# Weight sums and splits of the output products on pairs of tiles, temporaries in pools of each phase

## The chip, the cores and the metric

One core of one Trainium2 chip. The program is launched once; the metric is the device time of the launch in microseconds (us), median of three runs. TensorE (PE) multiplies, VectorE (DVE), ScalarE (ACT) and GpSimd (POOL) do the work on elements, and SyncE's queue (SP) issues most transfers. Each engine runs its instructions in the order in which the program lists them.

## The reference

Two residual layers on x[512 tokens, 2048]: a gated linear recurrence (mixer A, 16 heads of 128), then attention with forget gates (mixer B, 16 heads of 128). The change touches the last line of each layer, the output product:

```python
# layer A
h = rmsnorm(x, norm_w);  proj = h @ w_in            # queries, forget gates, values, gate
o = hgrn2_chunkwise(q, k, i, log_f)
o = head_rmsnorm(o, out_norm_w) * silu(gate)
x = x + o @ w_out                                    # [512, 2048] @ [2048, 2048]
# layer B
k, v, F = shared_kv(x, ...)
o = forgetting_attention(q, k, v, F)
o = head_rmsnorm(o, out_norm_w) * silu(gate)
x = x + o @ w_out
```

All is float32. The kernel splits each operand of a product in two float32r parts, a high and a low one (x = xh + xl, w = wh + wl), and adds three products: wh xh, wh xl, wl xh.

## The kernel before

**Tiling.** Everything is kept feature-major: a tile has 128 features as partitions and the 512 tokens as columns. A contraction over 2048 features has 16 tiles (kt = 0 to 15). A plain group (`group`) makes four output tiles at once, in four PSUM banks gm0 to gm3: for each kt one weight tile 128x512 is loaded (`Chunks.load`, SP queue, 256 KB, three buffers wr), split by a cast on ScalarE (wh) and a subtraction on VectorE (wl; both in `split`, L420 and L421), and used by twelve matmuls of 512 columns (L217 to L219 where the weights are stationary). Between the steps of a group the program interleaves the mixers of the heads (`pump`).

**Phases.** Phase "a" runs mixer A and its projections. The output product of A follows: its tiles 0 to 3 as one plain group, while the last heads finish (`out_product`), and its tiles 4 to 15 in "quick" form, phase "oa". Then phase "b" for mixer B, a plain group, and phase "ob" for the quick part of B's output product, which ends the program.

**The quick form.** Six groups u = 0 to 5 make two output tiles each, by Winograd's form of Strassen's product: seven products of half-size blocks in place of eight. Weight and operand are cut into four blocks (A11 to A22; B11 to B22). For each p = 0 to 7, a pair of contraction tiles p and p + 8, there is one weight tile 128x512 that holds the four blocks, and 21 matmuls of 256 columns (L268 to L270: seven products of three parts), so 168 a group. A group accumulates in four banks, gm and mx in turn. Around it stand:
- `w_sums` (L134 to L137) makes the four sums wm of the weight blocks: three additions on POOL and one on VectorE, 128x128 each, for each weight tile. `w_split_quick` then casts and subtracts the blocks (128x384) and the sums (128x512) into w7h and w7l.
- `quick_prep` (L234 to L237) makes, once for each p, the four sums tm of the operand's blocks: three on VectorE, one on POOL (L235), 128x256 each; then it splits the first into the place of half an operand tile (xh, xl) and the other three into th and tl (128x768). These serve all six groups. tm has one buffer. Preparations 0 to 3 are traced ahead of the plain group's last contraction tile, 4 to 7 in the first quick group.
- `quick_sum` (L278 to L289) puts the seven products of a group together and adds the residual: a copy on ScalarE, eleven operations of 256 columns on VectorE.
- The plain group's four banks are emptied by L806 (in A, result y) and L988 (in B, result z).

**What sets the order.** The program is traced in the order of the Python code, and the tile framework then schedules it: a simulated timeline decides, for each engine, in which order its instructions are listed. What it may move depends on the buffers: a tile that takes the space of another has to wait for it. Tiles of a mixer or of a quick product live in a pool of the phase (`mt`), opened by `phase`; those that live through all phases (t, wh, wl, wr, sl, vh, vl, the operands xh and xl, the y) in one pool of the program (`nt`). The space of a phase's pool is used again by the next phase's.

Of the kernel before, what the change touches and what calls it, by code (L numbers as in the profile page):

```python
# [15 lines left out]
P = 128  # L16
T = 512
# [14 lines left out]
def hgrn2_fox(ctx, tc, io):  # L32
# [24 lines left out]
    def tmp():  # L57
        return nt("t", (P, T), 4)
# [4 lines left out]
    def mt(tag, shape, bufs=1, dt=F32):  # L63
        """A tile of the phase's mixer."""
        return nt(tag, shape, bufs, dt, cur["sb"])

# [5 lines left out]
    def pump(n):  # L72
        """Trace n steps of the first two tasks in turn; the second starts when the first is halfway."""
# [56 lines left out]
    def w_sums(r):  # L130
        """Of the blocks A21, A11, A12, A22 the four sums of Winograd's form."""
        a21, a11, a12, a22 = (r[:, i * P : (i + 1) * P] for i in range(4))
        m = mt("wm", (P, 4, P), 2)
        G.tensor_add(m[:, 0, :], a21, a22)  # L134
        G.tensor_sub(m[:, 2, :], a11, a21)  # L135
        G.tensor_sub(m[:, 1, :], m[:, 0, :], a11)  # L136
        V.tensor_sub(m[:, 3, :], a12, m[:, 1, :])  # L137
        return m

    def w_split_quick(r, m):  # L140
        """A11, A12, A22 and the sums."""
        h = mt("w7h", (P, 7, P), 2, F32R)
        l = mt("w7l", (P, 7, P), 2, F32R)
        split(r[:, P:T].rearrange("p (a c) -> p a c", c=P), h[:, 0:3, :], l[:, 0:3, :])
        split(m, h[:, 3:7, :], l[:, 3:7, :])
        return h, l

    class Chunks:
        """The weight tiles of all groups in the order of their use."""
# [6 lines left out]
        def add(self, ap, scales):  # L156
            for kt in range(KT):
                self.todo.append((ap[kt], None, lambda r, m, kt=kt: w_split(r, kt, scales)))

        def add_quick(self, ap):  # L160
            for kt in range(KT // 2):
                self.todo.append((ap[kt], w_sums, w_split_quick))

        def load(self):
            if not self.todo:
                return
            ap, sums, fn = self.todo.pop(0)
            r = nt("wr", (P, T), 3)
            nc.sync.dma_start(r, ap)
            self.raw.append([r, sums, fn, None])  # L170

        def sums(self, n):
            for c in self.raw[:n]:
                if c[1] and cur["quick"]:
                    c[3] = c[1](c[0])
                    c[1] = None

        def split(self):
            if not self.raw:
                return  # L180
            self.sums(1)
            r, _, fn, m = self.raw.pop(0)
            self.parts.append(fn(r, m))
            self.sums(1)

        def take(self):
            while len(self.parts) < 2 and self.raw:
# [11 lines left out]
    def group(evac, token_major=False, rate=3, before=None):  # L199
        """Four accumulations over the contraction, one per bank."""  # L200
        banks = [nt(f"gm{j}", (P, T), 1, pool=ps) for j in range(4)]
        for kt in range(KT):
            wts.load()
            if before:
                before(kt)
            wts.split()
            h, l = wts.take()
            for j in range(4):
# [866 lines left out]
```

## Time and profile before

| | us |
|---|---|
| median of three runs | 2034.12 (2033.39 to 2034.17) |
| the profiled execution, first to last instruction | 2033.7 |
| A: first quick matmul, last matmul of group u = 4 | 911.75, 1023.1 |
| B: first quick matmul, last matmul | 1899.18, 2026.6 |

The times of the stretches come from one profiled execution. In the rows of the profile, `out<-in` names a tile that is written and those that are read (`w7l<-wr,w7h` is the low part of a quick weight), a bracket gives the idle time ahead of an instruction and what ended it, and L is the line in the kernel.

The six quick groups of A's product take 22.1, 22.0, 22.8, 22.6 and 22.2 us for u = 0 to 4, counted from the start of one to the start of the next; those of B's 22.9, 20.8, 21.3, 21.4, 20.4 and 20.8 us.

### The profile page before, as it was taken

Reading aid. Unit: us, or ns where it says so; the run is one execution under the profiler, and the core shown is the slowest. Engines: PE = TensorE matmul, PEld = TensorE weight load, DVE = VectorE, ACT = ScalarE, POOL = GpSimd, SP = SyncE. Lnnn points to the kernel's source line nnn. Section 1 sums busy time; section 2 is a strip of 40 time slices with the busy share of each in tenths; the row PEclk is TensorE's granted clock in tenths of the full one; section 3 lists DMA queues with packets and bytes.
Section 4 is the critical chain, followed back from the end, with each engine's and each line's share of the span. In section 5 each row is a group of like instructions: output and inputs, shape, how many; then the busy total and the mean of one; then the engine's idle time right before and its main releaser. Section 6 shows DMA issues by size and latency. Waiting matters only on the chain. (4 is left out here: it accounts for less than half of the span.)

```text
span 2033.7 us, 30490 instructions
## 1 busy us (share of the span) xinstructions
PE 1986.5 (98%) x10202; PEld 1693.6 (83%) x10202; DVE 1587.4 (78%) x3346; ACT 1142.1 (56%) x2408; POOL 481.1 (24%) x692
## 2 busy tenths in 40 slices
PE   7999999999999999989989999999999999999898
PEld 6888888888888888879987888888888888888898
DVE  8878987989799889798985667666766676687877
ACT  5656665667567465654453655554555456566443
POOL 8303210314033031147740000010001000011565
PEclk9999999999999999999999999999999999999999
DMA  5322222222222222244443333323323322323453
GB/s 174 84 82 83 68 84 78 79 78 78 78 80 71 82 80 78 89 118 137 147 125 89 94 94 88 91 87 99 92 85 94 94 89 88 92 80 107 132 157 114
DMA packets 107501, 195.14 MB, mean 96 GB/s; under 512 B 12992, under 2 KB 13120, under 8 KB 107344
## 3 DMA queue, kind: packets, MB, share of 16 engines
q1 hardware_dynamic: 107200, 193.19, 31.9%
q8 instruction: 80, 1.31, 0.3%
q14 instruction: 77, 0.63, 0.1%
q10 hardware_dynamic: 144, 0.01, 0.0%
HBM read 184.73 MB, written 8.42 MB: 95 GB/s over the span
## 5 line engine op out<-in xcount | busy, mean ns | idle before, releaser
L217 PE MATMUL gm<-xh,wh 128*128 128x512 f32 x1664 | 652.0, 392 | 6.8 <-ACT wh L420 6.6
L218 PE MATMUL gm<-xl,wh 128*128 128x512 f32 x1664 | 651.6, 392 | 0.0
L219 PE MATMUL gm<-xh,wl 128*128 128x512 f32 x1664 | 614.9, 392 | 6.3 <-DVE wl L421 5.8
L217 PEld LDWEIGHTS gm<-xh,wh 128*128 128x128 f32 x1664 | 313.6, 189 | 70.9 <-ACT wh L420 7.0
L219 PEld LDWEIGHTS gm<-xh,wl 128*128 128x128 f32 x1664 | 311.9, 188 | 70.9 <-DVE wl L421 7.2
L218 PEld LDWEIGHTS gm<-xl,wh 128*128 128x128 f32 x1664 | 313.6, 188 | 63.2
L421 DVE TENSOR_TENSOR wl<-wr,wh 128x512 fp32r<-128x512 f32 x288 | 216.6, 756 | 68.1 <-ACT wh L420 59.3
L420 ACT CAST wh<-wr 128x512 fp32r<-128x512 f32 x288 | 177.4, 620 | 150.5 <-PE gm L218 108.6
L125 DVE SCALAR_TENSOR_TENSOR wl<-wr,v_b_norm_w,wh 128x256 fp32r<-128x256 f32 (+1 forms) x192 | 113.1, 590 | 134.3 <-ACT wh L124 123.1
L124 ACT ACTIVATE wh<-wr,v_b_norm_w 128x256 fp32r<-128x256 f32 (+1 forms) x192 | 111.9, 585 | 181.7 <-PE gm L218 133.9
L214 PE MATMUL gm<-wl,xh 128*128 128x512 f32 x512 | 201.5, 394 | 0.0
L215 PE MATMUL gm<-wh,xl 128*128 128x512 f32 x512 | 200.0, 391 | 0.0
L213 PE MATMUL gm<-wh,xh 128*128 128x512 f32 x512 | 184.9, 392 | 1.1 <-DVE z L542 0.9
L919 POOL TENSOR_SCALAR_AFFINE_SELECT s<-s 128x128 f32<-128x128 f32 x64 | 27.5, 430 | 644.9 <-DVE s L918 644.2
L124 ACT ACTIVATE wh<-wr,v_kv_norm_w 128x256 fp32r<-128x256 f32 (+1 forms) x192 | 110.3, 574 | 59.0 <-PE gm L215 35.1
L125 DVE SCALAR_TENSOR_TENSOR wl<-wr,v_kv_norm_w,wh 128x256 fp32r<-128x256 f32 (+1 forms) x192 | 111.2, 581 | 35.7 <-ACT wh L124 35.1
L568 DVE COPY_PREDICATED at<-m,mx 128x128 f32<-128x128 uint8 (+3 forms) x448 | 109.6, 296 | 8.1 <-PE mx L575 7.6
L213 PEld LDWEIGHTS gm<-wh,xh 128*128 128x128 f32 x512 | 96.0, 188 | 21.1 <-DVE z L542 1.3
L214 PEld LDWEIGHTS gm<-wl,xh 128*128 128x128 f32 x512 | 96.3, 188 | 18.5 <-DVE wl L421 0.4
L215 PEld LDWEIGHTS gm<-wh,xl 128*128 128x128 f32 x512 | 96.2, 188 | 18.6
L370 POOL TENSOR_TENSOR z<-z,t 128x512 f32<-128x512 f32 x32 | 49.7, 1568 | 208.2 <-ACT t L369 208.1
L420 ACT CAST w7h<-wm 128x512 fp32r<-128x512 f32 x96 | 59.5, 620 | 66.0 <-DVE wm L137 65.3
(239 smaller groups left out, 4121.9 us busy)
## 6 DMA issues: line engine op xcount, KB each, us to landing
wr<-in_wa_qf SPq DMA_DIRECT2D x128, 256.0 KB, 2.6
wr<-in_wb_qk SPq DMA_DIRECT2D x128, 256.0 KB, 2.6
wr<-in_wa_v SPq DMA_DIRECT2D x64, 256.0 KB, 2.6
wr<-in_wa_g SPq DMA_DIRECT2D x64, 256.0 KB, 2.6
wr<-in_wb_v SPq DMA_DIRECT2D x64, 256.0 KB, 2.6
wr<-in_wb_g SPq DMA_DIRECT2D x64, 256.0 KB, 2.6
wr<-in_wa_q SPq DMA_DIRECT2D x48, 256.0 KB, 2.6
wr<-in_wb_q SPq DMA_DIRECT2D x48, 256.0 KB, 2.7
```

The lines of the kernel that those rows point to most:

```text
L124: S.activation(h[:, c], r[:, c], AF.Copy, scale=w[:, kt : kt + 1])
L125: V.scalar_tensor_tensor(l[:, c], r[:, c], w[:, kt : kt + 1], rd(h)[:, c], op0=ALU.mult, op1=ALU.subtract)
L213: PE.matmul(banks[j], xh, h, start=f, stop=False)
L214: PE.matmul(banks[j], xh, l, start=False, stop=False)
L215: PE.matmul(banks[j], xl, h, start=False, stop=e)
L217: PE.matmul(banks[j], h[:, c], Xh[kt], start=f, stop=False)
L218: PE.matmul(banks[j], h[:, c], Xl[kt], start=False, stop=False)
L219: PE.matmul(banks[j], l[:, c], Xh[kt], start=False, stop=e)
L370: G.tensor_mul(z, z, l)
L420: S.copy(h, src)
L421: return V.tensor_sub(l, src, rd(h))
L568: V.copy_predicated(out, mv, data)
```

## The change

- **Weight sums.** Two weight tiles are taken at a time. The sums are written in another, equivalent form of the seven products, so that all four come out of three VectorE additions on views of both tiles: one of 2x256 columns and two of 2x128 (L146 to L148). POOL has none of them left. The order of the blocks in the weights' memory layout changes with it.
- **Pairs of weight tiles.** All weights, those of the mixers too, come in loads of 512 KB for two tiles; wr has two buffers of that size in place of three of half. Quick weights are split in pairs (2x384 and 2x512 columns), into tiles wh and wl of two pairs. Lines: the matmuls of the plain group are L227 to L229, the quick ones L282 to L284, the split is L432 and L433, `quick_prep` L244 to L247, the evacuations L811 and L993.
- **Sums of the products.** `quick_sum` takes whole banks: a copy of 512 columns on ScalarE and seven operations on VectorE, three of 256 and four of 512 columns (L291 to L301).
- **Pools.** The temporaries t, sl, wh, wl, vh and vl are now allocated in the phase's pool, and the pools are opened with waits for single tiles. The mixers' pr has one buffer in place of two, and the norm's sum of squares takes the buffer of rstd.
- **Start.** The input tiles and the first weights are fetched in the order x0, x1, w0 and w1 together, x2, x3, instead of x0, w0, x1, w1, x2, w2, x3.

In numbers of instructions: POOL 698 before, 410 after; VectorE 3290 and 3201; ScalarE 2348 and 2251; DMAs issued by SP 749 and 429; matmuls the same.

```diff
@@ tmp, phase
     def tmp():
-        return nt("t", (P, T), 4)
+        return mt("t", (P, T), 4)
...
+        cur["sb"] = c.enter_context(tc.tile_pool(name=f"sb{name}", bufs=1, reuse_waits="tile"))
...
-        cur["sb"] = c.enter_context(tc.tile_pool(name=f"sb{name}", bufs=1))
@@ weights
+    def w_tiles(shape):
+        n = 2 if cur["quick"] else 3
+        return mt("wh", shape, n, F32R), mt("wl", shape, n, F32R)
...
     def w_sums(r):
-        a21, a11, a12, a22 = (r[:, i * P : (i + 1) * P] for i in range(4))
-        m = mt("wm", (P, 4, P), 2)
-        G.tensor_add(m[:, 0, :], a21, a22)
-        G.tensor_sub(m[:, 2, :], a11, a21)
-        G.tensor_sub(m[:, 1, :], m[:, 0, :], a11)
-        V.tensor_sub(m[:, 3, :], a12, m[:, 1, :])
+        m = mt("wm", (P, 2, 4, P), 2)
+        V.tensor_add(m[:, :, 0:2, :], r[:, :, 2:4, :], view(r, 0, [[4 * P, 2], [0, 2], [1, P]]))
+        V.tensor_add(m[:, :, 2, :], m[:, :, 0, :], r[:, :, 3, :])
+        V.tensor_add(m[:, :, 3, :], m[:, :, 2, :], r[:, :, 1, :])
         return m
...
-        split(r[:, P:T].rearrange("p (a c) -> p a c", c=P), h[:, 0:3, :], l[:, 0:3, :])
-        split(m, h[:, 3:7, :], l[:, 3:7, :])
-        return h, l
+        split(r[:, :, 1:4, :], h[:, :, 0:3, :], l[:, :, 0:3, :])
+        split(m, h[:, :, 3:7, :], l[:, :, 3:7, :])
+        return [(h[:, i, :, :], l[:, i, :, :]) for i in range(2)]
...
-            r = nt("wr", (P, T), 3)
+            r = nt("wr", (P, 2 * T), 2)
@@ quick_prep
-        G.tensor_sub(m[:, 2, :], b22, b12)
+        G.tensor_sub(m[:, 2, :], b12, b22)
         V.tensor_sub(m[:, 1, :], b22, m[:, 0, :])
-        V.tensor_sub(m[:, 3, :], m[:, 1, :], b21)
+        V.tensor_sub(m[:, 3, :], b21, m[:, 1, :])
@@ quick_sum
-        S.copy(u2, P1)
-        V.tensor_add(o1[:, lo], P1, r1[:, lo])
...
-        V.scalar_tensor_tensor(o2[:, lo], P4, -1.0, o2[:, lo], op0=ALU.mult, op1=ALU.add)
+        S.copy(e, p16)
+        V.tensor_sub(u, e[:, :TN], e[:, TN:])
+        V.tensor_sub(e[:, TN:], u, p45[:, TN:])
+        V.tensor_sub(u, p7[:, :TN], u)
+        V.tensor_add(e, p23, e)
+        d = tmp()
+        V.tensor_add(
+            d.rearrange("p (a c) -> p a c", a=2), p45.rearrange("p (a c) -> p a c", a=2), view(u, 0, [[0, 2], [1, TN]])
+        )
+        V.tensor_add(o1, e, r1)
+        V.tensor_add(o2, d, r2)
@@ Norm, mixers, start
-            self.acc = nt("vh", (P, T), 1)
+            self.acc = nt("rstd", (P, T), 1)
...
-        pr = mt("pr", (P, NW, 192), 2)
+        pr = mt("pr", (P, NW, 192), 1)
...
-    for kt in range(3):
+    for kt in range(2):
         fetch_x()
-        wts.load()
+    wts.load()
+    fetch_x()
     fetch_x()
```

How the order changes on VectorE is shown at three places. In the rows, the first number behind a name counts tiles.

The first is the end of A's plain group. Before, the evacuations L806 of its banks stand behind the preparation of p = 6 (tl6), and those of p = 0 to 5 stand further up, among the plain group's weight splits (wl):

```order
L236 TENSOR_TENSOR tm_2057_10111<-y14_1730_8512,tm_2057_10111 128x256
L421 TENSOR_TENSOR xl6_1967_9712<-tm_2057_10111,xh6_1966_9711 128x256
L237 TENSOR_TENSOR tm_2057_10111<-tm_2057_10111,y14_1730_8512 128x256
L421 TENSOR_TENSOR w7l_2047_10033<-wm_2028_9972,w7h_2046_10032 128x512
L137 TENSOR_TENSOR wm_2048_10038<-wr_2010_9907,wm_2048_10038 128x128
L421 TENSOR_TENSOR tl6_2059_10117<-tm_2057_10111,th6_2058_10116 128x768
L806 TENSOR_TENSOR y0_2029_9980<-gm0_1931_9573,z_1927_9565 128x512
L234 TENSOR_TENSOR tm_2064_10156<-y7_961_4690 128x256
L137 TENSOR_TENSOR wm_2055_10083<-wr_2042_10019,wm_2055_10083 128x128
L806 TENSOR_TENSOR y1_2030_9987<-gm1_1932_9574,z_1928_9567 128x512
```

In the changed program, the same place: the plain group's last two weight splits are wl_1867 and wl_1872, and the first row of the first preparation (tm_1875, of p = 0) comes next. L811 is the evacuation, wr_1868 and wr_1903 are the first two pairs of quick weights:

```order
L433 TENSOR_TENSOR wl_1867_9596<-wr_1859_9569,wh_1866_9595 128x512
L433 TENSOR_TENSOR wl_1872_9618<-wr_1859_9569,wh_1871_9617 128x512
L244 TENSOR_TENSOR tm_1875_9641<-y0_252_1248 128x256
L146 TENSOR_TENSOR wm_1887_9685<-wr_1868_9611 128x2x256
L146 TENSOR_TENSOR wm_1910_9782<-wr_1903_9737 128x2x256
L246 TENSOR_TENSOR tm_1875_9641<-y8_1056_5404,tm_1875_9641 128x256
L811 TENSOR_TENSOR y0_1890_9698<-gm0_1801_9313,z_1797_9305 128x512
L433 TENSOR_TENSOR wl_1889_9690<-wr_1868_9611,wh_1888_9689 128x2x384
```

All eight preparations have moved behind the plain group's last weight split, and the evacuations, which stood behind seven of them, are spread over the first four.

The second place is where the last of them ends, still in A and in the changed program: the preparations of p = 6 and 7, and the first rows behind.

```order
L433 TENSOR_TENSOR tl6_1916_9821<-tm_1914_9815,th6_1915_9820 128x768
L433 TENSOR_TENSOR wl_1930_9971<-wr_1927_9943,wh_1929_9970 128x2x384
L244 TENSOR_TENSOR tm_1917_9847<-y7_901_4570 128x256
L433 TENSOR_TENSOR wl_1930_9971<-wm_1928_9966,wh_1929_9970 128x2x512
L246 TENSOR_TENSOR tm_1917_9847<-y15_1705_8726,tm_1917_9847 128x256
L433 TENSOR_TENSOR xl7_1838_9466<-tm_1917_9847,xh7_1837_9465 128x256
L247 TENSOR_TENSOR tm_1917_9847<-y15_1705_8726,tm_1917_9847 128x256
L146 TENSOR_TENSOR wm_1949_10103<-wr_1948_10080 128x2x256
L147 TENSOR_TENSOR wm_1949_10103<-wm_1949_10103,wr_1948_10080 128x2x128
L433 TENSOR_TENSOR tl7_1919_9853<-tm_1917_9847,th7_1918_9852 128x768
L148 TENSOR_TENSOR wm_1949_10103<-wm_1949_10103,wr_1948_10080 128x2x128
```

From L244 of tm_1875 to tl7_1919 these are 74 rows on VectorE: 40 of the preparations, 20 weight sums, ten weight splits, and the four evacuations.

The third place is the same stretch in B. Before, as in A, the evacuations L988 stand behind tl6:

```order
L237 TENSOR_TENSOR tm_4114_20223<-tm_4114_20223,y14_3909_19274 128x256
L421 TENSOR_TENSOR w7l_4104_20145<-wm_4092_20098,w7h_4103_20144 128x512
L137 TENSOR_TENSOR wm_4105_20150<-wr_4074_20033,wm_4105_20150 128x128
L421 TENSOR_TENSOR tl6_4116_20229<-tm_4114_20223,th6_4115_20228 128x768
L988 TENSOR_TENSOR z_3991_19691<-gm0_3995_19699,z_3991_19691 128x512
L234 TENSOR_TENSOR tm_4121_20268<-y7_3231_16121 128x256
L137 TENSOR_TENSOR wm_4112_20195<-wr_4099_20131,wm_4112_20195 128x128
L988 TENSOR_TENSOR z_3992_19693<-gm1_3996_19700,z_3992_19693 128x512
L988 TENSOR_TENSOR z_3993_19695<-gm2_3997_19701,z_3993_19695 128x512
```

In the changed program the evacuations are L993, and the plain group's last weight splits wl_3699 and wl_3704:

```order
L433 TENSOR_TENSOR wl_3699_19090<-wr_3691_19063,wh_3698_19089 128x512
L433 TENSOR_TENSOR wl_3704_19112<-wr_3691_19063,wh_3703_19111 128x512
L993 TENSOR_TENSOR z_3629_18799<-gm0_3633_18807,z_3629_18799 128x512
L993 TENSOR_TENSOR z_3630_18801<-gm1_3634_18808,z_3630_18801 128x512
L993 TENSOR_TENSOR z_3631_18803<-gm2_3635_18809,z_3631_18803 128x512
L244 TENSOR_TENSOR tm_3707_19135<-y0_2289_12210 128x256
L146 TENSOR_TENSOR wm_3719_19179<-wr_3700_19105 128x2x256
L993 TENSOR_TENSOR z_3632_18805<-gm3_3636_18810,z_3632_18805 128x512
L146 TENSOR_TENSOR wm_3735_19262<-wr_3728_19217 128x2x256
L246 TENSOR_TENSOR tm_3707_19135<-y8_3008_15710,tm_3707_19135 128x256
L433 TENSOR_TENSOR wl_3721_19184<-wr_3700_19105,wh_3720_19183 128x2x384
```

Here three evacuations stand ahead of the first preparation (tm_3707), and all eight behind the plain group's last split.

More of the change, by code (lines that the diff above doesn't have):

```diff
@@ L65, in mt, with phase @@
         return nt(tag, shape, bufs, dt, cur["sb"])
+    def phase(name):
+        if cur:
+            cur["ctx"].close()
+        cur["ctx"] = c = ExitStack()
+        cur["quick"] = name[0] == "o"
+        cur["sb"] = c.enter_context(tc.tile_pool(name=f"sb{name}", bufs=1, reuse_waits="tile"))
+    phase("a")
     tasks = []
@@ L156, in add @@
         def add(self, ap, scales):
-            for kt in range(KT):
-                self.todo.append((ap[kt], None, lambda r, m, kt=kt: w_split(r, kt, scales)))
+            for k in range(KT // 2):
+                self.todo.append((ap[k], False, scales, 2 * k))
         def add_quick(self, ap):
-            for kt in range(KT // 2):
-                self.todo.append((ap[kt], w_sums, w_split_quick))
+            for k in range(KT // 4):
+                self.todo.append((ap[k], True, None, 0))
         def load(self):
@@ L166, in load @@
                 return
-            ap, sums, fn = self.todo.pop(0)
-            r = nt("wr", (P, T), 3)
+            ap, quick, scales, kt = self.todo.pop(0)
+            r = nt("wr", (P, 2 * T), 2)
             nc.sync.dma_start(r, ap)
[L170 to L176, printed above, removed]
-        def split(self):
[L179 to L184, printed above, removed]
+            if quick:
+                self.raw.append((lambda r=r.rearrange("p (a b c) -> p a b c", a=2, c=P): w_split_quick(r, w_sums(r)), 2))
+            else:
+                for i in range(2):
+                    self.raw.append((lambda v=r[:, i * T : (i + 1) * T], k=kt + i: [w_split(v, k, scales)], 1))
+        def split(self):
+            if self.raw:
+                fn, _ = self.raw.pop(0)
+                self.parts.extend(fn())
         def take(self):
-            while len(self.parts) < 2 and self.raw:
+            if not self.parts:
                 self.split()
@@ L202, in group @@
         for kt in range(KT):
-            wts.load()
+            if kt % 2 == 0:
+                wts.load()
             if before:
                 before(kt)
-            wts.split()
+            if not wts.parts:
+                wts.split()
             h, l = wts.take()
+            if not wts.parts:
+                wts.split()
             for j in range(4):
@@ L247, in quick @@
         for p in range(KT // 2):
-            wts.load()
+            if p % 2 == 0:
+                wts.load()
             if before:
                 before(p)
-            wts.split()
+            if not wts.parts:
+                wts.split()
             h, l = wts.take()
+            if not wts.parts:
+                wts.split()
             th, tl = prep[p]
@@ L441, in fetch_x @@
             nc.sync.dma_start(xs[kt], io["x"][kt])
-    for kt in range(3):
+    for kt in range(2):
         fetch_x()
-        wts.load()
+    wts.load()
+    fetch_x()
     fetch_x()
@@ L517, in hgrn2_fox @@
     setup.append(lambda: [V.memset(t, 0.0) for t in ats])
-    def phase(name):
-        if cur:
-            cur["ctx"].close()
-        cur["ctx"] = c = ExitStack()
-        cur["quick"] = name[0] == "o"
-        cur["sb"] = c.enter_context(tc.tile_pool(name=f"sb{name}", bufs=1))
-    phase("a")
     QA, KA, GA = [None] * H, [None] * H, [None] * H
@@ L844, in x1_split @@
             norm1.finish()
[L847 removed]
+    wf = mt("t", (P, KT, H), 4)
     nc.sync.dma_start(wf, io["wb_f"])
@@ L1017, in quarters @@
         b = w.reshape(2, 8, P, n, 2, P).transpose(3, 1, 2, 0, 4, 5)
-        b = np.stack([b[:, :, :, i, j] for i, j in ((0, 1), (0, 0), (1, 0), (1, 1))], 3)
-        return np.ascontiguousarray(b.reshape(n, 8, P, T))
+        b = np.stack([b[:, :, :, i, j] for i, j in ((0, 1), (1, 0), (1, 1), (0, 0))], 3)
+        b = b.reshape(n, 4, 2, P, T).transpose(0, 1, 3, 2, 4)
+        return np.ascontiguousarray(b.reshape(n, 4, P, 2 * T))
     def pairs(w1, w2, by_head):
```

48 lines of the change are left out of this document (18 added, 30 removed).

## The prediction

> **What bounds the kernel now.** I read the busy line first, then a table of stretches, then the timeline where TensorE stands still.
>
> ```profile
> PE 1986.5 (98%) x10202; PEld 1693.6 (83%) x10202; DVE 1587.4 (78%) x3346; ACT 1142.1 (56%) x2408; POOL 481.1 (24%) x692
> ```
> TensorE is busy for 98% of the span, so a gain can only come from the stretches where it is not. Columns of the next view: stretch, its length, then busy time and instructions of PE, PEld, DVE, ACT, POOL, then granted clock, DMA share and GB/s.
>
> ```profile
> 50.00:885.00 835.00, 826.54 (x4043) 698.24 (x4042) 710.08 (x1686) 508.61 (x1121) 180.75 (x238) 1.00 0.28 81
> 907.00:912.00 5.00, 0.81 (x4) 0.42 (x3) 4.85 (x11) 1.81 (x3) 3.71 (x7) 0.95 0.19 52
> 912.00:934.00 22.00, 21.82 (x171) 21.52 (x172) 17.42 (x29) 11.45 (x22) 15.73 (x22) 0.93 0.47 145
> 934.00:956.00 22.00, 21.31 (x172) 20.47 (x172) 20.44 (x35) 10.38 (x20) 17.46 (x26) 1.00 0.46 144
> 1001.00:1023.00 22.00, 21.31 (x170) 20.28 (x169) 20.56 (x36) 10.23 (x20) 16.96 (x27) 1.00 0.47 145
> 1057.00:1850.00 793.00, 792.46 (x3681) 657.51 (x3679) 534.74 (x1065) 438.35 (x929) 48.51 (x79) 1.00 0.31 91
> 1850.00:1893.50 43.50, 43.50 (x192) 35.56 (x192) 38.97 (x60) 27.73 (x51) 16.05 (x16) 1.00 0.38 116
> 1893.50:1899.00 5.50, 0.54 (x3) 0.12 (x1) 5.35 (x10) 1.45 (x2) 4.20 (x7) 0.90 0.26 86
> 1899.00:1922.00 23.00, 22.65 (x168) 22.45 (x169) 15.46 (x29) 9.22 (x17) 11.60 (x20) 0.87 0.48 161
> 1985.50:2006.00 20.50, 20.48 (x171) 20.14 (x170) 17.36 (x35) 9.16 (x18) 14.02 (x25) 1.00 0.47 149
> ```
> The mixers (50 to 885, 1057 to 1850) idle TensorE for 8.5 and 0.5 us. The quick output products run in six groups u = 0 to 5 of 168 matmuls each. At full clock TensorE needs about 0.120 us for one (20.5 / 171), 20.2 us a group. In A's product a steady group takes 22 us, with VectorE busy for 20.5 of them: there VectorE, slowed by POOL's 17 us, sets the pace. In B's product TensorE nearly does. Before each product stands a stall:
>
> ```profile
> 907.17 0.39 PE L219 MATMUL gm<-xh,wl 128*128 128x512 f32 x1
> 910.01 1.00 DVE L421 TENSOR_TENSOR tl<-tm,th 128x768 fp32r<-128x768 f32 x1
> 910.93 0.68 DVE L806 TENSOR_TENSOR y<-gm,z 128x512 f32<-128x512 f32 x1
> 911.75 0.55 PE L268 MATMUL gm<-xh,w7h 128*128 128x256 f32 x1 [4.19 <-POOL wm L136]
> 1893.66 0.39 PE L219 MATMUL gm<-xh,wl 128*128 128x512 f32 x1
> 1898.45 0.68 DVE L988 TENSOR_TENSOR z<-gm,z 128x512 f32<-128x512 f32 x1
> 1899.18 0.58 PE L268 MATMUL gm<-xh,w7h 128*128 128x256 f32 x1 [5.14 <-DVE z L988]
> ```
> The first quick matmul needs bank gm0, which L806 (L988 in B) empties, and that instruction is queued on VectorE behind the preparation of operands for the quick product (tl). The releaser named in the first bracket, POOL L136, is not the cause; the evacuation is what ended last.
>
> **The preparations move.** I call the start of the last plain matmul T: 907.17 in A, 1893.66 in B. Before, seven of the eight preparations (L234 to L237 and the splits to th, tl, xl) are done on VectorE ahead of the evacuations, mostly in shadow of the plain group, which is TensorE-bound. In the new order all eight stand behind the last weight split of the plain group, and the evacuations are spread among them: the new phase pool lies over the space of the phase before, which is now where wh, wl and t live. Each preparation uses the one buffer tm, so they are serial. Between the first L244 and the last tl, VectorE has 74 instructions in A. Prices, from rows of before:
>
> ```profile
> 894.53 0.96 DVE L234 TENSOR_TENSOR tm<-y 128x256 f32<-128x256 f32 x1
> 895.52 0.42 DVE L236 TENSOR_TENSOR tm<-y,tm 128x256 f32<-128x256 f32 x1
> L421 DVE TENSOR_TENSOR tl<-tm,th 128x768 fp32r<-128x768 f32 x16 | 15.4, 963 | 4.9 <-ACT th L420 4.6
> L806 DVE TENSOR_TENSOR y<-gm,z 128x512 f32<-128x512 f32 x4 | 2.6, 677 | 0.0
> L137 DVE TENSOR_TENSOR wm<-wr,wm 128x128 f32<-128x128 f32 x96 | 39.2, 409 | 29.4 <-POOL wm L136 29.3
> L421 DVE TENSOR_TENSOR w7l<-wr,w7h 128x384 fp32r<-128x384 f32 x96 | 72.5, 755 | 3.7 <-ACT w7h L420 3.7
> L420 ACT CAST th<-tm 128x768 fp32r<-128x768 f32 x16 | 13.4, 835 | 16.5 <-DVE tm L237 16.4
> L235 POOL TENSOR_TENSOR tm<-y,y 128x256 f32<-128x256 f32 x16 | 17.1, 1069 | 54.4 <-DVE tl L421 33.7 <-PE mx L416 17.4 <-DVE xl L421 2.6
> ```
> 256 columns cost 0.42, 512 cost 0.68, 768 cost 0.96: some 0.27 for each further 256. No row has 1024 columns (the wide weight split): it lies between 0.96 and two of 512, 1.36, and I take 1.23, one step on from the 0.96. For the two-row views (2x256, 2x128) I take the price of the flat shape with as many columns; they should not cost more than two halves apiece (0.42 twice for 2x256, 0.41 for 2x128, 0.755 for 2x384, 0.68 for 2x512), some 10 us more over the whole list.
> - 32 preparation rows of 256 (L244, L246, L247, xl): 13.4. Eight tl: 7.7.
> - Weight sums that stand among them: 7 L146 at 0.68, 13 L147 and L148 at 0.42: 10.2. Five pairs of weight splits at 0.96 + 1.23: 11.0.
> - Four evacuations: 2.7. Sum 45.0.
> - One row in each preparation runs beside POOL's L245 and pays 0.96 or 0.85 in place of 0.42: eight times 0.43, 3.4.
> - tl waits for ACT's cast th (0.84 us and about 0.2 to start). Four of the eight have no other row between, and wait about 1.05 each; I take 4.4 with one short one.
>
> That is 52.8 us. Only four rows (2.2 us) can run ahead of the first evacuation, which waits for gm0's last matmul, nine matmuls of 0.227 (43.5 / 192) before the last, plus its 0.39: released at T - 1.65. So the last tl is ready at **T - 1.65 + 52.8 - 2.2 = T + 49** in A. In B three evacuations stand ahead of the first L244. The third waits for gm2's last matmul, three before the end (T - 0.3), and takes 0.68, so the list starts at T + 0.4; without those three (2.0) and with one L148 more (0.42) it is 51.2 us: about **T + 51**.
>
> Until then TensorE can only do the matmuls ahead of the first that reads tl7: 201 of 1008, some 24 us of work. 807 are left. In A the fifth group's end frees what follows; in B the sixth's.
>
> ```profile
> 1022.68 0.40 PE L270 MATMUL gm<-xh,w7l 128*128 128x256 f32 x2
> 2026.35 0.28 PE L270 MATMUL mx<-th,w7l 128*128 128x256 f32 x1
> 1904.70:1922.00 17.30, 17.13 (x144) 16.93 (x144) 10.71 (x20) 7.98 (x15) 10.48 (x18) 1.00 0.50 166
> ```
>
> - After the last tl, a group of the new form costs VectorE 4 x (0.68 + 0.42 + 0.42 + 0.96 + 1.23) = 14.8 for four pairs of weight tiles and 3 x 0.42 + 4 x 0.68 = 4.0 for the sums of L291 to L301: 18.8, below TensorE's 20.2, and POOL's three weight sums, which slowed VectorE, are gone. I take 20.4 a group, with a little waiting.
> - The clock. In the next stretches TensorE runs at half its clock and takes 0.21 us a matmul:
>
> ```profile
> 1037.80:1044.50 6.70, 5.57 (x26) 5.57 (x27) 5.16 (x9) 2.60 (x6) 3.52 (x7) 0.50 0.28 81
> 1899.20:1904.70 5.50, 5.50 (x26) 5.50 (x27) 4.55 (x9) 1.24 (x2) 0.93 (x2) 0.50 0.43 151
> ```
> While TensorE waits for tl the half clock costs nothing: 201 x 0.21 = 43 us is under 49. What is left of a slow stretch behind the last tl costs 0 to 3.3 us (half of the longest, 6.7); I take 1.7.
> - A: 49 + 639 / 168 x 20.4 (= 77.6) + 1.7 = T + 128.3. Before, that group ended at 1023.08, T + 115.9: **+12.4**.
> - B: 51 + 807 / 168 x 20.4 (= 98.0) + 1.7 = T + 150.7. Before, the last matmul ended at 2026.63, T + 133.0: **+17.7**.
>
> The evacuation stalls (4.2 and 5.1 us) and the faster groups are in these sums, as gains; without them it would be worse.
>
> By the Trainium skill, "TensorE: Matmul & The Clock Gate", Part 1, the clock drops to half after about 3.4 us of idling and comes back after as long a busy window. By that page the bursts of 21 matmuls between two preparations (2.5 us of work in 6) might never bring the full clock back before the last tl, and one whole window of about 3.4 us would follow; an estimate from it would lose 1.7 us at half clock, as my term has it. The trace agrees on the half clock behind a stall; its slow stretches of 5.5 and 6.7 us are longer than one window of that page, and two windows would make the sum 2069. By "VectorE: DVE Perf Modes", The TRN2 errata, fewer and larger instructions save a fixed cost each, which speaks for this change: the price rows above agree (0.68 for 512 against twice 0.42), and it is in my steady group; it cannot reach the order of the instructions.
>
> **The other edits.**
> - Start: the first weight load is twice as large (512 KB) and one x tile goes ahead of it.
>
> ```profile
> 1.25 0.42 SPq L169 DMA_DIRECT2D wr<-in_wa_qf  x1
> 5.57 2.08 PE L217 MATMUL gm<-xh,wh 128*128 128x512 f32 x4 [5.57 <-ACT wh L420]
> wr<-in_wa_qf SPq DMA_DIRECT2D x128, 256.0 KB, 2.6
> ```
> Between 0.5 (one issue later) and 0.5 + 2.6 (the second 256 KB takes as long as the first): I take +1.5. Later loads have a pair's time, 24 matmuls of 0.227 or 5.4 us, and the first half is not split before the whole has landed; still two buffers ahead of need, so 0.
> - Mixers: the same instructions, another order, pr with one buffer, waits of single tiles in place of whole pools. TensorE's 8.5 idle us are all there is to gain; VectorE's 125 idle us in 50 to 885 cover some 48 extra waits for pr of 1.1 us (a cast and a subtraction). Taken as 0, bounds -5 to +8.
> - The switch from A's product to B's mixer and the tail: seven sums after the last matmul in place of eleven, but wider, 4.0 against 11 x 0.41 = 4.5, and ACT's copy is twice as long. 0, bounds -3 to +3.
>
> **Sum.** 12.4 + 17.7 + 1.5 = 31.6 on the span of 2033.7: 2065.3. The runs have a median of 2034.12, 0.4 more than that span: **2066 us**.
>
> **Rivals.**
> 1. *The steady groups gain nothing* (VectorE's wide rows cost more than extrapolated, or the weights come late). They then stay at 22 us in A and 20.9 in B (1922 to 2026.63 for its last five): A T + 49 + 83.7 + 1.7, +18.5; B T + 51 + 100.4 + 1.7, +20.1; total 2074. For it: no row shows 1024 columns. Against: POOL is all but out of the groups.
> 2. *The burst is short, and the change wins.* The whole list between L244 and tl7 is what matters: break-even is the last tl at T + 115.9 - 77.6 - 1.7 = T + 36.6 in A and T + 33.3 in B. It would need 12 to 18 us of the list done in the shadow of the plain group, as before. If all preparations were, TensorE would set the pace from T on: A 5 x 20.4 = T + 102, -13.9; B 6 x 20.4 = T + 122.4, -10.6; total 2011, faster. Against it: VectorE goes in order, and the evacuation L811 of gm0 is the fifth row of the list, so nothing behind it can be early. The cheapest prices (1024 columns at 0.96, no contention, ACT hidden) give T + 40 and T + 42, and with groups at 20.2 a total of 2046, still not faster.
> 3. *The half clock outlasts the burst.* If TensorE stays at half clock for a whole slow stretch of 6.7 us behind the last tl, each product loses 3.3 in place of 1.7: 2069. For it: TensorE is idle half of the time until then. This is also what the Trainium skill's page on the clock gate would give with two windows.
> 4. *The mixers lose* (new order, single pr): +8 to +15 beside the forecast, 2074 to 2081. Against: VectorE's idle time in both.
> 5. *Gains and burst cancel.* Stalls gone and faster groups against a burst that ends near T + 37 and T + 34. Part of the list would have to be early, which the order speaks against as in 2.
>
> **How the numbers follow.** Forecast 0.48; rival 1 0.18; rival 3 0.12; rival 4 0.10; rival 2 0.08; rival 5 0.04. The forecast's own prices reach from 2046 (the cheapest, above) to about 2092 (two-row views at two halves, +10 a product; start and switch dear, +5). From 2046 to 2086 lies some 0.8: left out are rivals 2 and 5 and the dearest ends of 1 and 4. Within 0.2% (4 us, about what a measurement of this kernel can tell): 0.04; faster 0.08; slower 0.88.
>
> **What would show it.** In the profile after: TensorE idle for some 25 us in the first 49 behind the last plain matmul of both products, in pieces released by VectorE's tl; the last tl at T + 49 and T + 51; no stall at the first quick matmul longer than 2 us; steady groups of 20 to 21 us with POOL nearly idle; the first matmul near 7 us. I am wrong if the last tl comes before T + 37, if groups stay at 22, or if the mixers' lengths (835 and 793) change by more than 8 us.

## The result, and the profile after

The changed kernel takes 2090.99 us, median of four runs (2088.61 to 2092.97), against 2033.76 us for the kernel before (four runs, 2033.11 to 2034.17). The ratio is 1.028 (95% interval 1.0265 to 1.0294): slower, as forecast, but by 57 us where 32 were forecast, and outside the range of 2046 to 2086.

The busy line of the changed kernel:

```profile
PE 2028.2 (97%) x10202; PEld 1701.7 (81%) x10202; DVE 1579.0 (76%) x3250; ACT 1132.6 (54%) x2312; POOL 316.1 (15%) x404
```
The same number of matmuls as before keeps TensorE busy for 42 us longer. That is the first sign that the loss isn't only waiting. (VectorE's instructions are 3346 before and 3250 after by the profiles; the section on the change counts them as 3290 and 3201.) The span divides at the start of the last plain matmul (T), at the end of the quick group u = 4 of A, at the first matmul of mixer B's groups and at the last matmul of all. Times from the traces, in us; two experiments of below stand beside the two kernels (columns 3 and 4: the weights of the kernel before displaced by 32 bytes; the changed kernel with its weights put back in place):

| stretch | before | after | e2_before_w32 | e6_congruent |
|---|---|---|---|---|
| start to T of A | 907.2 | 921.2 | 918.4 | 909.0 |
| T of A to the end of u = 4 | 115.9 | 127.1 | 114.2 | 127.9 |
| to the first matmul of B | 33.6 | 34.5 | 33.1 | 32.8 |
| to T of B | 836.9 | 857.6 | 853.9 | 840.0 |
| T of B to the last matmul | 133.0 | 144.8 | 131.3 | 144.1 |
| to the end | 7.0 | 6.1 | 7.0 | 6.1 |
| span | 2033.7 | 2091.2 | 2057.8 | 2059.8 |

The quick products lose 11.2 and 11.8 us; the plain stretches, for which the prediction had 1.5 us at the start and nothing else, lose 14.0 and 20.7.

**The quick products.** Timelines of TensorE and VectorE of the changed kernel, at T of A and at the last tl of A and of B (start, duration, engine, line, what):

```profile
921.15 0.40 PE L229 MATMUL gm<-xh,wl 128*128 128x512 f32 x1
921.39 0.28 PE L282 MATMUL gm<-xh,wh 128*128 128x256 f32 x1
...
966.91 0.95 DVE L433 TENSOR_TENSOR tl<-tm,th 128x768 fp32r<-128x768 f32 x1
...
1940.32 0.40 PE L229 MATMUL gm<-xh,wl 128*128 128x512 f32 x1
1940.55 0.28 PE L282 MATMUL gm<-xh,wh 128*128 128x256 f32 x1
...
1987.22 0.96 DVE L433 TENSOR_TENSOR tl<-tm,th 128x768 fp32r<-128x768 f32 x1 [0.17 <-ACT th L432]
```
The stall ahead of the first quick matmul is gone (0.24 us from the last plain one), and the last tl is ready at T + 46.7 and T + 47.9. The table of stretches, from the first quick matmul to the last tl of A, and two later groups of A and B:

```profile
921.20:925.30 4.10, 0.76 (x6) 0.51 (x4) 3.82 (x9) 1.89 (x3) 0.00 (x0) 1.00 0.20 71
925.30:938.90 13.60, 8.63 (x34) 7.46 (x35) 12.56 (x20) 4.58 (x7) 5.29 (x4) 0.50 0.29 111
938.90:956.00 17.10, 12.30 (x91) 10.99 (x90) 15.62 (x26) 7.30 (x11) 4.52 (x4) 1.00 0.34 108
956.00:962.80 6.80, 6.28 (x25) 5.70 (x26) 5.28 (x8) 3.39 (x5) 2.32 (x2) 0.50 0.00 0
962.80:968.00 5.20, 5.20 (x46) 5.20 (x45) 4.57 (x9) 1.24 (x2) 0.03 (x1) 1.00 0.36 101
...
985.70:1005.60 19.90, 19.90 (x171) 19.90 (x170) 17.77 (x29) 8.99 (x12) 6.67 (x2) 1.00 0.46 143
2004.50:2024.40 19.90, 19.90 (x170) 19.90 (x170) 17.19 (x29) 8.00 (x10) 0.00 (x0) 1.00 0.51 154
```
VectorE is busy for 41.9 of the 46.8 us while TensorE gets some 200 matmuls done, part of them at half clock (0.50 in the third column from the end). The slow stretches are over before the last tl. The two later groups in the last rows take 19.9 us with TensorE busy throughout, so the wide sums do what they say there.

**The plain groups.** One stretch of 700 us from the middle of mixer B's groups, of before and of after. TensorE is busy for the whole of it in both, so the number of matmuls is the pace:

```profile
1100.00:1800.00 700.00, 700.00 (x3262) 582.60 (x3261) 469.03 (x949) 390.12 (x837) 37.71 (x70) 1.00 0.31 91
```

```profile
1100.00:1800.00 700.00, 700.00 (x3189) 569.59 (x3188) 446.77 (x907) 373.17 (x804) 35.41 (x64) 1.00 0.29 89
```
2.2% fewer matmuls in the same busy time, at the same full clock, and no releaser to name: TensorE waits for nobody. The distance from the start of one 512-column matmul of the plain groups to the next (gaps over 300 ns left out) has a mean of 228.7 ns before and 233.8 after, over some 6,440 of them; 5.1 ns on each are 33 us. The most frequent value before is 227 ns, in the changed kernel 235.

### The profile page after: what moved, and what is told of

It is laid out like the page before. It is cut to its first block, busy times and chain, and to the rows that moved or that the text cites. A ratio compares the mean times of both kernels' runs of the same rounds, so it can differ in the third digit from the quotient of the medians.

```text
span 2091.2 us, 28900 instructions
## 1 busy us (share of the span) xinstructions
PE 2028.2 (97%) x10202; PEld 1701.7 (81%) x10202; DVE 1579.0 (76%) x3250; ACT 1132.6 (54%) x2312; POOL 316.1 (15%) x404
## 4 chain that ended last, share of the span: by engine, by line
PE 83%; DVE 7%; DMA 3%; ACT 2%; issue 2%; POOL 2%; SPq 0%; DVEq 0%; ACTq 0%; POOLq 0%
PE gm L227 17%; PE gm L229 17%; PE gm L228 17%; PE gm L224 5%; PE gm L223 5%; PE gm L225 5%; DVE wl L433 3%; DMA wr<-in_wb_q 2%; PE mx L580 1%; PE mx L579 1%; PE mx L578 1%; PE mx L427 1%; PE mx L428 1%; PE mx L284 1%; PE mx L426 1%
## 5 line engine op out<-in xcount | busy, mean ns | idle before, releaser
L227 PE MATMUL gm<-xh,wh 128*128 128x512 f32 x1664 | 662.0, 398 | 13.9 <-ACT wh L432 8.3
L228 PE MATMUL gm<-xl,wh 128*128 128x512 f32 x1664 | 661.8, 398 | 0.0
L229 PE MATMUL gm<-xh,wl 128*128 128x512 f32 x1664 | 625.6, 398 | 5.7 <-DVE wl L433 5.5
L227 PEld LDWEIGHTS gm<-xh,wh 128*128 128x128 f32 x1664 | 314.3, 189 | 86.5 <-ACT wh L432 8.3
L229 PEld LDWEIGHTS gm<-xh,wl 128*128 128x128 f32 x1664 | 312.1, 189 | 77.6 <-DVE wl L433 7.0
L432 ACT CAST wh<-wr 128x512 fp32r<-128x512 f32 (+1 forms) x336 | 217.3, 649 | 232.5 <-PE gm L228 125.8
L433 DVE TENSOR_TENSOR wl<-wr,wh 128x512 fp32r<-128x512 f32 (+1 forms) x336 | 261.8, 783 | 107.7 <-ACT wh L432 101.5
L573 DVE COPY_PREDICATED at<-m,mx 128x128 f32<-128x128 uint8 (+3 forms) x448 | 106.6, 296 | 13.6 <-PE mx L580 13.0
L432 ACT CAST kh<-k 128x512 fp32r<-128x512 f32 (+1 forms) x96 | 56.4, 587 | 52.0 <-PE mx L579 25.8
L382 POOL TENSOR_TENSOR z<-z,t 128x512 f32<-128x512 f32 x32 | 47.9, 1509 | 237.0 <-ACT t L381 236.9
```

Of the source, the lines that this page charges most:

```text
L227: PE.matmul(banks[j], h[:, c], Xh[kt], start=f, stop=False)
L228: PE.matmul(banks[j], h[:, c], Xl[kt], start=False, stop=False)
L229: PE.matmul(banks[j], l[:, c], Xh[kt], start=False, stop=e)
L382: G.tensor_mul(z, z, l)
L432: S.copy(h, src)
L433: return V.tensor_sub(l, src, rd(h))
```

## The experiments

What differs for those matmuls? The weight parts wh and wl moved from the common pool, between the operands, into the phases' pools behind them. Before, every tile of wh, wl, xh and xl starts at the same place modulo 2048 bytes in its partition. After, the last tile of the common pool is the 16-byte column of 1/rms, and the phases' pools start 32 bytes off that grid. The first four runs ask whether this sets the pace, and whether the burst of preparations is due to the weight buffers.

**e1_aligned.** In the changed kernel:

```diff
-            self.col = nt("rstdc", (P, NW, 1), 1)
+            self.col = nt("rstdc", (P, 16, 1), 1)[:, 0:NW, :]
```


> The changed kernel with one tile of the common pool (the column of 1/rms) made 64 bytes long instead of 16, so that all that lies behind it, the weight parts wh and wl among it, starts 32 bytes later and on a multiple of 64 bytes. Nothing else differs. Theory 1 (alignment: a weight tile that starts at 32 modulo 64 bytes makes every 512-column matmul of the plain groups longer): their mean distance goes back from 233.7 to about 228.5 ns, and 6500 of them give 2091 - 33 = 2057 us. Theory 2 (the pace is lost to something else that the change brings, the 512 KB loads for instance): 233.7 ns and 2091 us stay. The quick groups behave as in the changed kernel under both: last tl at T + 47.

Measured: 2088.13 us (ratio to before 1.0261, 1.0244 to 1.0278), mean distance 233.0 ns. A start on a multiple of 64 bytes isn't what counts; theory 1 falls in this form.

**e2_before_w32.** In the kernel before, 32 bytes ahead of wh and 32 behind wl:

```diff
+        if not Xh[1]:
+            G.memset(nt("pad0", (P, 8), 1), 0.0)
         h = nt("wh", (P, T), 3, F32R)
         l = nt("wl", (P, T), 3, F32R)
+        if not Xh[1]:
+            G.memset(nt("pad1", (P, 8), 1), 0.0)
```


> The kernel before with a 32-byte tile ahead of the buffers of wh and one behind those of wl: wh and wl alone start at 32 modulo 64, the operands xh and xl stay on multiples of 64, all else as before. Theory 1 (alignment): the plain groups' distance goes from 228.5 to about 234 ns, 2034 + 33 = 2067 us. Theory 2 (512 KB loads or another part of the change): no difference, 2034 us.

Measured: 2059.20 us (1.0124, 1.0109 to 1.0139), mean distance 233.8 ns, and the same stretch of 700 us:

```profile
1100.00:1800.00 700.00, 700.00 (x3193) 569.56 (x3192) 456.95 (x920) 378.89 (x812) 36.08 (x66) 1.00 0.30 89
```
So 32 bytes between the places of weights and operands, and nothing else of the change, bring the changed kernel's pace. The two tiles also move all that lies behind wl by 64 bytes, so the operands of kt 0 start 32 bytes below the weights and those of kt 1 to 15 32 bytes above; the median is 234 ns for every kt. 512 KB loads are not needed for it. The total grew by 25 us, not 33: by the first table 11.2 and 17.0 in the plain stretches, and 3.4 come back in the quick ones.

**e5_before_all32.** In the kernel before, a 32-byte constant ahead of all:

```diff
+    G.memset(const("pad", (P, 8)), 0.0)
     eps = const("eps", (P, 1))
```


> The kernel before with a 32-byte constant ahead of everything: weights and operands alike start at 32 modulo 64. If the start of each tile alone counts (theory 1a): at least as slow as with the weights displaced alone, 2067 us or more. If only the difference between operand and weight counts (theory 1b): 228.5 ns and 2034 us. Theory 2: 2034 us.

Measured: 2036.03 us (1.0009, 0.9999 to 1.0018), 228.7 ns, and the 700 us:

```profile
1100.00:1800.00 700.00, 700.00 (x3262) 582.32 (x3261) 467.93 (x947) 388.89 (x835) 37.59 (x70) 1.00 0.30 91
```
Theory 1b holds: the place of a tile doesn't count, the distance between weights and operands does.

**g1_weights_common_pool.** In the changed kernel:

```diff
-        n = 2 if cur["quick"] else 3
-        return mt("wh", shape, n, F32R), mt("wl", shape, n, F32R)
+        if cur["quick"] and len(shape) > 2:
+            return mt("wqh", shape, 2, F32R), mt("wql", shape, 2, F32R)
+        return nt("wh", shape, 3, F32R), nt("wl", shape, 3, F32R)
...
-        m = mt("wm", (P, 2, 4, P), 2)
+        m = mt("wm", (P, 2, 4, P), 1)
...
-        return mt("t", (P, T), 4)
+        return mt("t", (P, T), 3 if cur["quick"] else 4)
```


> The changed kernel with wh and wl of the plain groups in three buffers each of the common pool again, as before the change (and there on multiples of 64 bytes); to make room, wm has one buffer instead of two and t three instead of four in the quick phases. The preparations of p = 0 to 5 stand ahead of the evacuations again on VectorE. My theory of the burst (the preparations came behind the plain group because the new pool waits for the weight buffers): last tl near T + 7 instead of T + 47, TensorE starts at once, the first five groups of A end near T + 105 instead of 127, those of B near T + 125 instead of 145: 42 us less; with theory 1 on the pace 33 less again: about 2016 us. If the burst is not the cause of the slow first group, the groups stay and 2057 us come out; if the pace has another cause, 2049.

Measured: 2050.15 us (1.0075, 1.0060 to 1.0090). The pace is back (228.7 ns). The last tl comes at T + 22, not T + 7, and the stall for the evacuation is back with 5.0 us in A and 5.6 in B. From T to the end of u = 4 in A it takes 119.8 us, to the last matmul in B 140.5: 7 and 4 less than in the changed kernel, not 22 and 20. What TensorE waits for in A's groups 1 to 4:

```profile
PE mx L283 <- ACT wqh L433: 5.1, 2, 2.5
PE gm L283 <- ACT wqh L433: 1.3, 1, 1.3
```
The casts of the quick weights are late: the one buffer wm, which this edit needed for room, made a new wait.

**e6_congruent.** In the changed kernel, the 16-byte column moves to the constants, so that weights and operands are a multiple of 1024 bytes apart:

```diff
-            self.col = nt("rstdc", (P, NW, 1), 1)
+            self.col = nt("rstdc", (P, NW, 1), 1, pool=cp)
```


> The changed kernel with the column of 1/rms in the pool of constants instead of the common pool, so that the phases' pools start 32 bytes nearer to the operands: all of wh and wl lie a multiple of 1024 bytes away from xh and xl (before the change: a multiple of 2048; after it, that and 32 more; in the run with a 64-byte column, 64 more). Theory 1b (what counts is the distance of weight and operand, modulo some power of two above 64): mean distance of the plain matmuls 228.5 ns again, the plain stretches 28 us shorter as the displaced weights made them longer, 2091 - 28 = 2063 us; the burst stays, last tl at T + 47. Theory 2 (another part of the change): 233.7 ns, 2091 us; the run that displaced only the weights of the kernel before already speaks against it.

Measured: 2064.63 us (1.0153, 1.0136 to 1.0170), mean distance 228.5 ns.

```profile
1100.00:1800.00 700.00, 700.00 (x3261) 582.24 (x3261) 462.73 (x935) 384.97 (x824) 36.28 (x67) 1.00 0.29 91
```
One moved tile gives 26 us back in the medians (31 between the two profiled spans), nearly all of it in the plain stretches. What is left against before is the forecast's own subject: 12.0 us in A's quick product, 11.1 in B's, by the first table.

**e7_sweep.** In the kernel before, with one buffer for pr, small tiles between the operands:

```diff
+    PADS = {4: 8, 5: 8, 6: 8, 7: 8, 8: 8, 9: 8, 10: 8, 11: 8, 12: 16, 13: 16, 14: 16, 15: 16}
     def new_x(kt):
+        if not Xh[kt] and kt in PADS:
+            G.memset(nt(f"pad{kt}", (P, PADS[kt]), 1), 0.0)
```


> The kernel before with 32- or 64-byte tiles between the operands, so that xh and xl of contraction tile kt lie at 0 (kt 0 to 3), 32, 64, 96, 128, 160, 192, 224, 256, 320, 384, 448 and 512 bytes (kt 4 to 15) from the weights' place modulo 2048; pr has one buffer to make room. Theory 1b: the distance of the matmuls depends on kt: 227 ns where the displacement is a multiple of the power of two that counts, 234 elsewhere; 32 and 64 are slow by the runs so far; 128, 256 and 512 show which one it is. If the displacement acts on anything but the matmul's own two reads, all kt are alike.

Distance of the matmuls whose columns are xh or xl, by the place of that operand against the weights that are loaded next, modulo 2048 bytes (some 300 each; 1,570 at 0, where some 370 with the weights as columns are counted too):

| bytes | 0 | 32 | 64 | 96 | 128 | 160 | 192 | 224 | 256 | 320 | 384 | 448 | 512 |
|---|---|---|---|---|---|---|---|---|---|---|---|---|---|
| median ns | 227 | 234 | 229 | 234 | 232 | 234 | 233 | 232 | 227 | 231 | 232 | 233 | 228 |
| mean ns | 228.4 | 234.1 | 230.0 | 234.8 | 233.5 | 234.1 | 233.5 | 233.4 | 230.1 | 230.8 | 233.0 | 233.6 | 230.8 |

By the medians the pattern repeats with 256 bytes: fast at 0, 256 and 512, between at 64 and 320, slow at the others. By the means, 256 and 512 stay 2 ns above 0. In the kernel before, the median is 227 ns for every kt, so it isn't kt itself that counts. The kernel ran once, at 2051.2 us. Own weights and next weights have the same place in it, so it can't tell which of the two counts.

**e8_wl_only32 and e9_wl_only32.** Which two reads meet? Both displace wl alone in the kernel before. In e8, 32 bytes ahead of wl and 32 behind:

> The kernel before with a 32-byte tile between the buffers of wh and those of wl (and one behind): wl alone is displaced by 32 bytes against the operands, wh is not. In the plain groups with stationary weights the matmuls come as (xh, wh), (xl, wh), (xh, wl). Theory a (the read of a matmul's columns meets the load of the next weights): only the matmul ahead of one with wl, during which wl is loaded, is slow (234), the one with wl itself is fast (227), as the next load is of wh. Theory b (the matmul's own weights count): the one with wl is slow. Theory c (neither, the writes of the splits count): all three alike. About a third of the 28 us either way, some 2043 us.

It ran once, at 2055.06 us, and all three kinds are at 231 to 233 ns. The tiles of kt 1 to 15 had moved by 64 bytes against wh as well, so the three theories can't be told apart by it. In e9, 2016 bytes stand behind wl, and pr has one buffer:

```diff
         h = nt("wh", (P, T), 3, F32R)
+        if not Xh[1]:
+            G.memset(nt("pad0", (P, 8), 1), 0.0)
         l = nt("wl", (P, T), 3, F32R)
+        if not Xh[1]:
+            G.memset(nt("pad1", (P, 504), 1)[:, 0:8], 0.0)
```


> The run that displaced wl alone moved the operands of kt 1 to 15 by 64 bytes as well, so it told nothing. Here wl alone lies 32 bytes off: behind wl stand 2016 bytes more, so that xh, xl and wh keep their places modulo 2048; pr has one buffer to make room. Matmuls with stationary weights, by the weights they use and those loaded next. Theory a (the columns' read meets the load of the next weights): (own wh, next wl) and (own wl, next wl) slow, 233 or more, (own wl, next wh) 228. Theory b (its own weights): those with own wl slow, whatever comes next. Theory c (the stream as a whole, the splits' writes for instance): all alike, in between.

It ran once, at 2058.03 us. Mean distance: xl with own wh, next wl, 237.6 ns (1,304 matmuls); xh with own wl, next wh, 230.3 (1,334), and next wl, 232.9 (223); own wh, next wh, 229.0 with xl and 232.0 with xh. The slow ones are those during which the displaced wl is loaded, not those that use it: theory a carries most of it. The others are 1 to 4 ns above the 228 of the kernel before, which theory a doesn't give; that part stays open.

**g3_tm_in_wm, g4_mx_first_in_b, g6_start_as_before.** Three steps from g1 towards a version without the burst. g3:

```diff
-        m = mt("wm", (P, 2, 4, P), 1)
+        m = mt("wm", (P, 2, 4, P), 2)
...
-        m = mt("tm", (P, 4, TN), 1)
+        m = mt("wm", (P, 4, TN), 2)
```


> As the run with wh and wl in the common pool, but tm takes its place from the two buffers of wm, so wm has two buffers again. Theory: that run's groups were held at 22 to 24 us by the one buffer wm (ScalarE waited for the sums, TensorE for ScalarE); with two they take 20.3 us as in the changed kernel. A: five groups and the wait for the evacuation, T + 5 + 5 x 20.4 = T + 107 (T + 120 with one buffer), B: T + 5 + 6 x 20.4 = T + 128 (T + 140.5); total 2050 - 25 = 2025 us, below the kernel before. If the burst had moved into the groups and wm were not the cause, 2050 stays.

Measured: 2035.34 us (1.0010, 1.0000 to 1.0019): the same as before. The last tl comes at T + 17.9 in A, and A and B take 117.9 and 131.1 us from T: 10 and 13 less than in e6. Timelines of VectorE and of TensorE of g3, in A:

```profile
929.11 0.95 DVE L434 TENSOR_TENSOR tl<-wm,th 128x768 fp32r<-128x768 f32 x1
```

```profile
912.20 0.39 PE L230 MATMUL gm<-xh,wl 128*128 128x512 f32 x1
915.61 0.58 PE L283 MATMUL gm<-xh,wqh 128*128 128x256 f32 x1 [3.02 <-DVE y L812]
```
A's later groups take 20 to 22 us, but group u = 0 takes 29 (behind the 3.0 us for the evacuation). Its stretches, in TensorE's columns and clock:

```profile
915.60:921.70 6.10, 6.09 (x28) 6.09 (x29) 6.07 (x8) 4.26 (x7) 4.07 (x4) 0.50 0.79 252
921.70:931.90 10.20, 7.88 (x67) 7.67 (x65) 10.17 (x16) 3.70 (x5) 3.07 (x2) 1.00 0.15 56
931.90:938.75 6.85, 5.42 (x25) 5.42 (x26) 5.72 (x10) 1.99 (x2) 0.00 (x0) 0.50 0.44 153
938.75:944.70 5.95, 5.95 (x52) 5.95 (x51) 3.43 (x6) 2.38 (x3) 0.00 (x0) 1.00 0.29 85
```
Two slow stretches, one at the wait for the evacuation and one at a wait of 3.8 us for quick weights, hold 53 of its matmuls. At 0.21 us in place of 0.12 these cost about 5 us; with the 3.8 us and the 20.2 of a group at full clock that is the 29.

g4 is g3 with the banks of B's groups in the other order:

```diff
-                banks = [nt(f"gm{j}", (P, T), 1, pool=ps) if u % 2 == 0 else bank() for j in range(4)]
+                banks = [nt(f"gm{j}", (P, T), 1, pool=ps) if (u % 2 == 0) == (name == "oa") else bank() for j in range(4)]
```


> The run before it with one more edit: in B's product the groups u = 0, 2, 4 use the banks mx and the others gm, so that the first quick matmul doesn't wait for the evacuation of gm. Theory (the stall ahead of the quick groups is the evacuation, queued on VectorE behind preparations): B's stall of 5.4 us goes, 5 us less, 2020 us. If the operands or weights are late as well, the stall moves to the first th or wl and less than 2 us is gained.

Measured: 2037.10 us (1.0015, 1.0005 to 1.0024). TensorE starts 0.24 us after T in B and then waits inside the group:

```profile
PE mx L283 <- ACT wqh L433: 8.1, 2, 6.7
```
The stall moved to the weights; nothing is gained.

g6 is g3 with the start's loads in the order x0, w0 and w1, x1, x2, x3:

```diff
-    for kt in range(2):
-        fetch_x()
-    wts.load()
-    fetch_x()
     fetch_x()
+    wts.load()
+    for kt in range(3):
+        fetch_x()
```


> The run with tm in the buffers of wm, with the start's loads in the order x0, w0 and w1, x1, x2, x3 (the first weights are the second transfer again, but still 512 KB). Theory (the first matmul is late by 2.8 us since the first weights come one transfer later and are twice as large): 0.5 us come back if only the order counts, up to 1.5; 2033.5 to 2035 us, no difference from the kernel before that can be told.

Measured: 2036.80 us (1.0011, 1.0002 to 1.0020). The first matmul comes at 5.67 us instead of 8.36, more than expected, yet T of A moves from 912.2 to 911.9 only. A later wait takes up the rest.

**b1_mx_first_in_b.** The kernel before, with g4's edit alone.

> The kernel before with one edit: in B's product the groups u = 0, 2, 4 use the banks mx and the others gm, so the first quick matmul need not wait for the evacuation L988, which stands behind tl6 on VectorE. Theory (in the kernel before the stall of 5.1 us is that evacuation alone): TensorE starts within 1 us of the plain group's end, and VectorE, 4 to 5 us ahead of need in that group, does not hold it later: 4 to 8 us less, 2027 to 2030 us, faster than both kernels. If weights or preparations are due at the same time, the stall comes back inside the first group, as in the changed kernel with the same edit: 2034 us.

Measured: 2031.77 us, median of ten, against 2033.96 (0.9989, 0.9979 to 0.9999): less than both kernels, by two of the expected four to eight us, with an interval that just leaves out 1. TensorE at T of B:

```profile
1891.74 0.40 PE L219 MATMUL gm<-xh,wl 128*128 128x512 f32 x1
1891.97 0.28 PE L268 MATMUL mx<-xh,w7h 128*128 128x256 f32 x1
```
The stall is gone, so it was the evacuation; the first group then takes 25.4 us instead of 22.9, with waits of 3 us for quick weights. From T to the last matmul it is 130.6 us in place of 133.0.

## Why the prediction was wrong

Its sign held, and so did the mechanism of the burst. The larger part of the loss, 35 of 57 us, lies in the plain stretches, where it had forecast next to nothing.

- **The step that failed: "Mixers: the same instructions, another order ... Taken as 0, bounds -5 to +8."** It counted what TensorE could wait for and took the length of its matmuls from before as given; its first reading, "so a gain can only come from the stretches where it is not" busy, rests on the same. The length didn't stay: the plain stretches lost 14.0 and 20.7 us, and 12.2 and 17.6 of them went with e6, which moves one 16-byte tile. e2 shows the same loss in the kernel before. The prediction had the pools' new places in hand, and used them only for what waits for what. Rival 4 had the sign of this, less than half of its size, and the wrong cause (order, pr). Its sign of being wrong, mixers longer by more than 8 us, is the one that came.
- **The burst: right.** Last tl forecast for T + 49 and T + 51, measured at T + 46.7 and T + 47.9. The preparations stand behind the plain group and TensorE has some 200 matmuls done by then (201 forecast). e6 shows the cost alone, and g3, where they are early again, has 10 and 13 us of it back, though not in the way expected. Unlike forecast, TensorE was not idle for some 25 us in this time but for 13.6 in A (33.2 busy of 46.8): 20 of the 47 us ran at half clock, which cost next to nothing, as the prediction said: in A the first matmul that reads the last tl starts at 968.77, without a wait, 0.9 us after that tl is ready, and in B it waits 0.3 us for it. So in A TensorE itself, and no longer VectorE, was last by 0.9 us.
- **A's term: +12.4, measured +11.2** (127.1 against 128.3 forecast): 2.3 us from the earlier tl and 1.7 from the clock were gained on it, and 2.8 given back: 0.9 because TensorE had 194 matmuls started at the last tl and not 201, the rest by slower groups, 20.8 us in the mean for u = 1 to 4, the last of them 22.5.
- **B's term: +17.7, measured +11.8, mis-sized by 6 us:** the list 3.1 us shorter, groups of 20.2 us instead of 20.4 (1.1), and no slow stretch behind the last tl (1.7). Its start was also rounded down: T + 0.4 and a list of 51.2 us are T + 51.6, and T + 51 was carried on.
- **The prices.** The form that no row had shown, 128x1024, was taken at 1.23 us:

```profile
L433 DVE TENSOR_TENSOR wl<-wm,wh 128x1024 fp32r<-128x1024 f32 x48 | 59.5, 1239 | 0.3 <-ACT wh L432 0.3
L146 DVE TENSOR_TENSOR wm<-wr 128x512 f32<-128x512 f32 x48 | 35.8, 745 | 21.6 <-DMA wr<-in_wa_q 11.8 <-DMA wr<-in_wb_q 9.3
```
  It is 1.239. The two-row views cost hardly more than flat ones: for the 2x256 of L146 the median is 0.691 against 0.68, and some slower ones raise the mean to 0.745. The idle time in the second row, 21.6 us over both products, is VectorE waiting for the 512 KB loads, which the prediction had not counted; in the burst it is 0.6 us in A and 0.9 in B.
- **The start: +1.5, in effect 0.** The first matmul came 2.7 us later, but TensorE waits in the first group anyway and goes on at the same time in both kernels (before, then after):

```profile
37.13 1.22 PE L219 MATMUL gm<-xh,wl 128*128 128x512 f32 x3 [4.13 <-DVE wl L421]
```

```profile
36.95 1.36 PE L229 MATMUL gm<-xh,wl 128*128 128x512 f32 x4 [4.10 <-DVE wl L433]
```
  The term should have been followed to the next wait that ends later anyway.
- **Rivals.** Rival 1 (groups gain nothing) fell: 19.9 to 20.7 us, but for one of 22.5. Rivals 2 (short burst) and 5 (gains and burst cancel) fell with the last tl at T + 46.7. Rival 3: the slow stretches lasted longer than I took them to (13.6 us in A), but ended before the last tl. By the Trainium skill, "TensorE: Matmul & The Clock Gate", Part 1, the clock goes by windows of 3413 ns; the trace agrees, with slow stretches of 3.4, 6.8 and 13.6 us in the two products.

Without the displacement (e6) the changed kernel takes 2064.6 us; the forecast was 2066. That is closer than its terms were, and partly luck: B's was over 6 us too large, and what e6 leaves in the plain stretches is 4.9 us (1.8 and 3.1), within the bounds given for them and not the 1.5 that were taken. Where these 4.9 us come from, no run shows.

## What to carry to other kernels

When tiles change pools, look at their places as well as at their waits: print where the tiles that TensorE reads together start, and keep them on the same place modulo 256 bytes, or better a larger power of two, as e6 does with 1024 (a single 16-byte tile ahead of a pool moved 6,500 matmuls off it here). A stretch in which TensorE is busy throughout isn't safe from a change: compare the number of matmuls in a window of full busy time. And a delay at a place counts only up to the next wait that would end later anyway.

## What the runs showed of the hardware

- A 512-column float32r matmul here is followed by the next one after 227 or 228 ns (median) when its columns and the weights that are loaded next start at the same place modulo 256 bytes, and mostly after 232 to 234 ns when they don't (e7). In between lies one case: the columns start 64 bytes above the next weights' place, 229 ns, and 231 at 320 bytes (e7). 64 bytes below, as for most matmuls of e1, the mean is 234; e1's others, whose columns are the weights, lie 64 above and have 230. A displacement of both together has no effect (e5). That the next weights count, and not the matmul's own, rests on e9 alone.
- For the 256-column matmuls of the quick groups the same rule doesn't show: their mean (gaps over 150 ns left out) is 118.4 ns before, 118.5 in the changed kernel, 116.9 in e1, and 119.9 in e6, where all weights and operands are at the same place modulo 256.
- Which memory or port the two reads share, no run shows. e9 shows only that the matmul during which the displaced weights are loaded pays most.
